# Seven block products for eight in the up projection of a hybrid decoder layer

## The chip, the cores and the metric

The kernel runs on one NeuronCore of one Trainium2 chip. The metric is the device time of one execution in microseconds (us). Its engines have queues of their own and run beside each other: PE (matrix products), DVE and ACT (elementwise work), POOL (elementwise work too), and SP, which here issues the loads. Products are summed in PSUM, 8 banks of 128 x 512 f32; all else lies in SBUF.

## What is computed

One decoder layer on 256 tokens with 2048 features: an input projection, a state-space scan and a windowed attention beside it, an output projection, a feed-forward part with a causal convolution of three taps, and a gate on a projected per-layer embedding. The change is in the last three lines here and in what surrounds them:

```python
h = h + jnp.concatenate([y_ssm, y_att], axis=-1) @ w_out[i]
u = _rmsnorm(h, ffn_norm_g[i]) @ w_up[i]          # 2048 x 11264
u = _causal_dwconv(u, ffn_conv_w[i], ffn_conv_b[i])
g_ff, u_ff = jnp.split(u, [D_FF], axis=-1)        # D_FF = 5632
h = h + (jax.nn.silu(g_ff) * u_ff) @ w_down[i]
gate = jax.nn.sigmoid(_rmsnorm(h, ple_norm_g[i]) @ w_ple_gate[i])
pe = _rmsnorm(p[i] @ w_ple_proj[i], ple_post_g[i])
h = h + gate * pe
```

## The kernel before

Tokens lie in two blocks b of 128. Every f32 product is made of three products in the faster fp32r type: each operand is split into a rounded part hi and the rest lo, and hi x hi, hi x lo and lo x hi are summed in one PSUM bank (`products`, L222 to L224). A weight tile `w` has two K tiles (of 128 rows) by 512 columns, 512 KB, and is loaded by SP (L207, 7 buffers); ACT copies it to `wh` (L192), DVE subtracts to get `wl` (L193); `wh` and `wl` have 4 buffers. One tile feeds 2 K tiles x 2 blocks x 3 = 12 matmuls of 512 columns.

The feed-forward part walks over 11 pairs. A pair is one chunk of 512 gate columns (g) and one of 512 value columns (u). `up(c)` multiplies the left operand `hT` (the residual stream, transposed and scaled by the norm's gain; 16 K tiles) with one chunk's 8 weight tiles, 96 matmuls, into one PSUM pair. ACT scales the rows by `rh` on the way out (L879). Then the chunk is transposed: POOL copies the 16-bit halves of each number apart (`half`, L881), SP starts a DMA transpose to `flip`, POOL puts the halves together (`uc`, L884). ACT and DVE make the convolution (L286, L288: 8 DVE steps a chunk), ACT the SiLU, POOL the product of the two chunks (L904), and ACT and DVE split it into `gT` (`gh`, `gl`).

`project` multiplies `gT` with the rows of w_down for a segment of two pairs (the last has one): 4 column blocks, each in a PSUM pair that DVE adds to the residual `h` (L396). It runs one segment late, behind the ups of the segment that follows. While the output projection w_out ends, `next_lhs` squares the rows of `h` on ACT and transposes them on PE for `hT`; the row scale `rh` is known after the last of them and is applied behind the up. After the last `project`, `embed` makes the embedding's projection (48 matmuls), and the gate projection follows.

Of PSUM, `ps_acc` has two pairs (4 banks) and `ps_tr` two banks through the whole kernel. The order on each engine is made by a scheduler when the kernel is built; only in parts marked by `manual_schedule` PE keeps the order of the code. The queues of DVE, ACT and POOL run strictly in the order given.

## Time and profile before

| | |
|---|---|
| runs | 1434.60, 1434.63, 1436.28 us; median 1434.63 |
| profiled execution, span | 1434.9 us |
| DMA | 292.62 MB, mean 204 GB/s; HBM read 268.32 MB |
| PE busy, slice by slice | over 98% in every stretch of 100 us from 0 to 1300 |
| DVE busy in 100 us | 61 to 82 us |
| POOL busy in 100 us | 12 to 34 us between 600 and 1300, up to 48 in the attention part |
| the feed-forward part | from about 618 to 1317 us, then the embedding and the gate |

How to read the profile's rows: a line of kernel.py, the engine and its operation, what it writes and reads with partitions x elements, the count, then the busy time and the mean of one in ns, then the idle time of the engine just before and who ended it. In a timeline a row begins with its start and its length in us; equal neighbours are merged (x2). The length of an instruction includes what it waits for once it has been started, so the lone length of an operation and its length beside others differ. Matmuls overlap: their distance from start to start tells the rate, not their length.

### The profile page before, as it was taken

The page shows a single profiled execution, that of the slowest core. Times are in us where ns is not written, and L with a number is a line of the kernel's source. Part 1 is how long each engine was busy: PE and PEld are TensorE (multiplying, and loading weights), DVE is VectorE, ACT ScalarE, POOL GpSimd, SP SyncE. Part 2 cuts the span into 40 slices and gives each one's busy share as a digit, 9 for nine tenths or more (in the row PEclk, how much of TensorE's full clock was granted, in tenths as well). Part 3 has the DMA queues.
Part 4 walks back from the last instruction along what each step waited for, and adds up shares of the span by engine and source line. Part 5 has one row for each costly group of instructions (what it writes and reads, how often), then busy time and mean ns, then how long its engine had stood idle before and what let it go on. Part 6 is the DMA issues. An engine that isn't in the chain of part 4 may idle for free.

```text
span 1434.9 us, 18092 instructions
## 1 busy us (share of the span) xinstructions
PE 1423.2 (99%) x6527; PEld 1167.3 (81%) x6527; DVE 984.1 (69%) x1242; ACT 804.2 (56%) x1101; POOL 286.2 (20%) x212
## 2 busy tenths in 40 slices
PE   9999999999999999999999999999999999999998
PEld 7887888888787778888888888888888888888887
DVE  6678876776678897656667646765675576476854
ACT  6675555644567666556556446545554554455643
POOL 0002010008345432013243112201320131120000
PEclk9999999999999999999999999999999999999999
DMA  9656656548687778577887767867876877776671
GB/s 332 236 173 198 215 177 185 171 148 223 188 220 187 209 220 220 168 211 207 219 226 202 217 205 206 225 196 198 230 208 192 223 201 218 206 208 190 208 226 65
DMA packets 163467, 292.62 MB, mean 204 GB/s; under 512 B 93041, under 2 KB 95921, under 8 KB 162993
## 3 DMA queue, kind: packets, MB, share of 16 engines
q1 hardware_dynamic: 162944, 290.99, 70.5%
q8 instruction: 51, 0.84, 0.2%
q10 hardware_dynamic: 432, 0.48, 0.1%
q14 instruction: 40, 0.32, 0.1%
HBM read 268.32 MB, written 2.13 MB: 188 GB/s over the span
## 4 chain that ended last, share of the span: by engine, by line
PE 68%; DVE 1%; ACT 0%; issue 0%; POOL 0%; DVEq 0%; ACTq 0%
PE acc L222 22%; PE acc L224 22%; PE acc L223 22%; PE tr L779 1%; PE tr L272 0%; PE sc L738 0%; DVE wl L193 0%; ACT s L753 0%; DVE nm L749 0%; DVE s L742 0%; ACT wh L192 0%; DVE sg L931 0%; ACT s L761 0%; DVE qkr L672 0%; DVE h L396 0%
## 5 line engine op out<-in xcount | busy, mean ns | idle before, releaser
L193 DVE TENSOR_TENSOR wl<-w,wh 128x1024 fp32r<-128x1024 f32 (+1 forms) x495 | 634.9, 1288 | 378.5 <-ACT wh L192 376.4
L192 ACT CAST wh<-w 128x1024 fp32r<-128x1024 f32 (+1 forms) x495 | 514.8, 1045 | 480.7 <-PE acc L224 431.4
L223 PE MATMUL acc<-wl,ah 128*128 128x512 f32 x1278 | 500.1, 391 | 1.5 <-DVE wl L193 1.5
L224 PE MATMUL acc<-wh,al 128*128 128x512 f32 x1278 | 499.0, 391 | 0.0
L222 PE MATMUL acc<-wh,ah 128*128 128x512 f32 x1278 | 498.3, 392 | 0.0
L223 PEld LDWEIGHTS acc<-wl,ah 128*128 128x128 f32 x1278 | 240.1, 188 | 52.3 <-DVE wl L193 2.4
L222 PEld LDWEIGHTS acc<-wh,ah 128*128 128x128 f32 x1278 | 240.1, 188 | 51.0 <-issue 1.4
L224 PEld LDWEIGHTS acc<-wh,al 128*128 128x128 f32 x1278 | 240.1, 188 | 50.1 <-issue 0.7
L224 PE MATMUL acc<-wh,gl 128*128 128x512 f32 x352 | 137.1, 390 | 0.0
L223 PE MATMUL acc<-wl,gh 128*128 128x512 f32 x352 | 137.1, 390 | 0.0
L222 PE MATMUL acc<-wh,gh 128*128 128x512 f32 x352 | 136.5, 390 | 0.0
L881 POOL COPY half<-u 128x1024 uint16<-128x1024 uint16 x44 | 62.0, 1422 | 264.3 <-ACT u L879 264.3
L222 PE MATMUL acc<-wh,yh 128*128 128x512 f32 x256 | 101.6, 397 | 0.6 <-DVE h L396 0.6
L223 PE MATMUL acc<-wl,yh 128*128 128x512 f32 x256 | 99.9, 390 | 0.0
L224 PE MATMUL acc<-wh,yl 128*128 128x512 f32 x256 | 99.7, 390 | 0.0
L884 POOL COPY uc<-flip 128x1024 uint16<-128x1024 uint16 x44 | 54.9, 1248 | 177.2 <-DMA flip<-half 174.9
L223 PEld LDWEIGHTS acc<-wl,gh 128*128 128x128 f32 x352 | 66.1, 188 | 13.7
L224 PEld LDWEIGHTS acc<-wh,gl 128*128 128x128 f32 x352 | 66.1, 188 | 13.6
L222 PEld LDWEIGHTS acc<-wh,gh 128*128 128x128 f32 x352 | 66.1, 188 | 13.6
L288 DVE SCALAR_TENSOR_TENSOR cv<-uc,fcw,cv 128x254 f32<-128x254 f32 (+1 forms) x176 | 73.2, 476 | 3.4 <-ACT cv L286 3.4
L396 DVE TENSOR_TENSOR h<-h,acc 128x512 f32<-128x512 f32 x112 | 73.0, 678 | 1.8 <-PE acc L224 1.8
L222 PEld LDWEIGHTS acc<-wh,yh 128*128 128x128 f32 x256 | 48.1, 188 | 14.6 <-issue 2.0
(239 smaller groups left out, 1129.2 us busy)
## 6 DMA issues: line engine op xcount, KB each, us to landing
w<-in_w_up_dram SPq DMA_DIRECT2D x176, 512.0 KB, 4.2
w<-in_w_in_dram SPq DMA_DIRECT2D x126, 512.0 KB, 4.2
w<-in_w_down_dram SPq DMA_DIRECT2D x88, 512.0 KB, 4.3
w<-in_w_out_dram SPq DMA_DIRECT2D x64, 512.0 KB, 4.2
w<-in_w_pg_dram SPq DMA_DIRECT2D x32, 512.0 KB, 4.3
seg<-scr SPq DMA_DIRECT2D x8, 512.0 KB, 5.0
xt<-in_xT_dram SPq DMA_DIRECT2D x16, 128.0 KB, 7.0
h<-in_x_dram SPq DMA_DIRECT2D x2, 1024.0 KB, 8.7
```

The costliest lines, as they stand in the source:

```text
L192: S.copy(hi, src)
L193: V.tensor_tensor(out=lo, in0=src, in1=hi.bitcast(F32), op=ALU.subtract)
L222: PE.matmul(acc[b], lhsT=hi, rhs=wh[:, i, :], start=(k == 0), stop=False)
L223: PE.matmul(acc[b], lhsT=hi, rhs=wl[:, i, :], start=False, stop=False)
L224: PE.matmul(acc[b], lhsT=lo, rhs=wh[:, i, :], start=False, stop=(k == total - 1 or (b == NB - 1 and k + 1 == whole)))
L288: V.scalar_tensor_tensor(out=dst[:, s:], in0=ps[:, : T - s], scalar=taps[n - 1 - s], in1=dst[:, s:], op0=ALU.mult, op1=ALU.add)
L396: V.tensor_tensor(out=hs, in0=hs, in1=acc[b], op=ALU.add)
L779: PE.matmul(v3(o[e * HD : (e + 1) * HD, kv * 2 * P : (kv + 1) * 2 * P], 2), lhsT=v[kb][:, vs], rhs=pT[e][:, :, kb, :], start=(kb == 0), st ...
L881: G.tensor_copy(half.rearrange("p (a n) -> p a n", a=2), u_.bitcast(U16).rearrange("p (n a) -> p a n", a=2))
L884: G.tensor_copy(uc[:, :, b * P : (b + 1) * P].bitcast(U16).rearrange("p f (t a) -> p f t a", a=2), flip.rearrange("p (a f) t -> p f t a", ...
```

## The change

The up projection is made for both chunks of a pair at once, in cells of 2 K tiles. For a **mixed** cell the product of 2 token blocks x 2 K tiles with 2 K tiles x 2 chunks is a product of 2 x 2 blocks, and is made with 7 block products in place of 8, each with its three parts: 21 matmuls for 24. The other cells, every second one, are **plain** and keep 8. A pair has 4 of each: 180 matmuls where there were 192.

- The right-hand sums of the mixed cells: `ta` (wu0 - wg0, wu1 - wu0) and `tb` (wu1 - ta0, wg1 - tb0), four subtractions of 128 x 512, on POOL; for the first pair the first of them is on DVE. `wg`, `ta`, `tb` and half of `wu` (`v`) are then split on ACT and DVE.
- The left-hand sums are made once, in `left`, on DVE.
- One up takes all eight PSUM banks (P1, P6, P7, P5 for the mixed cells alone, Q2, Q4, Q3, Q22 for both kinds). Behind it ACT copies P1, and DVE makes eight additions that combine the banks. POOL and SP transpose the results as before.
- The rows are scaled by `rh` before they are transposed (`norm`, then `left`), so that nothing is scaled behind the up. The four `left` steps stand at the start of the part, between plain cells; the embedding's 48 matmuls are put there too, and its result goes to HBM and is read back before the gate.
- Down follows every up, two column blocks each, from the third pair on.
- PE has the order of the code from here to the end. A common pool `ps8` of 8 banks takes the place of `ps_acc` and `ps_tr`.

```diff
-    ps_acc = ctx.enter_context(tc.tile_pool(name="ps_acc", bufs=2, space=PSUM))
-    ps_tr = ctx.enter_context(tc.tile_pool(name="ps_tr", bufs=2, space=PSUM))
+    mixer = ExitStack()
+    ps_acc = mixer.enter_context(tc.tile_pool(name="ps_acc", bufs=2, space=PSUM))
+    ps_tr = mixer.enter_context(tc.tile_pool(name="ps_tr", bufs=2, space=PSUM))
...
+    banks = []
+
+    def bank():
+        return banks[0].tile([P, NC], F32, tag="b", name=nm("b"))
...
+    def load_raw(src):
 
         w = sb(wp, [P, KW, NC], "w", bufs=WR)
+        nc.sync.dma_start(w.rearrange("p a b -> p (a b)"), src)
+        return w
+
+    def split_w(w):
+
         wh = sb(wp, [P, KW, NC], "wh", F32R)
         wl = sb(wp, [P, KW, NC], "wl", F32R)
-        n = kt * NC // pieces
-        w2, wh2, wl2 = (t.rearrange("p a b -> p (a b)") for t in (w, wh, wl))
-        for i in range(pieces):
-            s = slice(i * n, (i + 1) * n)
-            nc.sync.dma_start(w2[:, s], src[:, s])
-            split(w2[:, s], wh2[:, s], wl2[:, s])
+        split(w, wh, wl)
         return wh, wl
+
+    def load_w(src):
+        return split_w(load_raw(src))
...
-    def next_lhs(lhs, ss, n, gain):
+    def squares(ss, n):
 
         for b in range(NB):
             sq = sb(small, [P, NC], "hsq")
             S.activation(out=sq, in_=hres[b][:, n * NC : (n + 1) * NC], func=AF.Square, accum_out=ss[:, b, n : n + 1])
+
+    def next_lhs(lhs, n, gain):
...
-            at[98 + 2 * n] = lambda n=n: next_lhs(hT, ssh, n, g_ffn)
+            at[98 + 2 * n] = lambda n=n: squares(ssh, n)
...
-        next_lhs(hT, ssh, 3, g_ffn)
+        squares(ssh, 3)
...
+        def embed(n):
             acc = acc_pair()
-            gemm(acc, plhs, [w_pe[n, g] for g in range(2 // KW)])
+            gemm(acc, lambda k, b: (ph[:, k, b * P : (b + 1) * P], pl[:, k, b * P : (b + 1) * P]), [w_pe[n, 0]])
             for b in range(NB):
-                pc = pe[b][:, n * NC : (n + 1) * NC]
-                V.tensor_copy(pc, acc[b])
-                sq = sb(small, [P, NC], "hsq")
-                S.activation(out=sq, in_=pc, func=AF.Square, accum_out=ssp[:, b, n : n + 1])
-
-    with tc.tile_pool(name="ffn", bufs=2) as fp:
-
-        def up(c):
-            acc = acc_pair()
-            gemm(acc, hT, [w_up[c, g] for g in range(KT // KW)])
+                t = staged(n % 2 * 2 + b)
+                V.tensor_copy(t, acc[b])
+                nc.scalar.dma_start(pe_d[b, :, n * NC : (n + 1) * NC], t)
...
+        def norm(n):
+            t = sb(fp, [P, NB, NC], f"cv{n % 2}", bufs=1)
+            for b in range(NB):
+                hs = hres[b][:, n * NC : (n + 1) * NC]
+                if n:
+                    S.activation(out=t[:, b, :], in_=hs, func=AF.Copy, scale=rh[:, b : b + 1])
+                else:
+                    V.tensor_scalar_mul(t[:, b, :], hs, rh[:, b : b + 1])
+            normed.append(t)
...
+        def left(n):
+
+            src = normed[n]
+
+            def flip(half):
+                tr = bank().rearrange("p (a t) -> p a t", a=2)
+                for i in range(2):
+                    f = half * 2 + i
+                    for b in range(NB):
+                        PE.transpose(tr[:, i, b * P : (b + 1) * P], src[:, b, f * P : (f + 1) * P], ident)
+                return tr
+
+            tr = flip(1)
+            h, l = (sb(fp, [P, 2, T], f"p{e}{n}", F32R, 1) for e in "hl")
+            for i in range(2):
+                k = 4 * n + 2 + i
+                split(tr[:, i, :], h[:, i, :], l[:, i, :], g_ffn[:, k : k + 1])
+            plain.append((h, l))
+            F = sb(fp, [P, 4, T], "uc", bufs=1).rearrange("p f (a t) -> p (f a) t", a=2)
+            tr = flip(0)
+            for i, dst in ((0, F[:, 0:8:7, :]), (1, F[:, 1:3, :])):
+                k = 4 * n + i
+                S.activation(out=dst, in_=v3(tr[:, i, :], 2), func=AF.Copy, scale=g_ffn[:, k : k + 1])
+            for o, x0, x1, op in ((3, 7, 2, ALU.add), (4, 3, 0, ALU.subtract), (5, 0, 7, ALU.subtract), (6, 1, 4, ALU.subtract)):
+                V.tensor_tensor(out=F[:, o, :], in0=F[:, x0, :], in1=F[:, x1, :], op=op)
+            hi, lo = (sb(act, [P, KG * T], f"a{e}{n}", F32R)[:, : 7 * P].rearrange("p (f t) -> p f t", f=7) for e in "hl")
+            split(F[:, :7, :], hi, lo)
+            mixed.append((hi, lo))
...
+        P1, P6, P7, P5, Q2, Q4, Q3, Q22 = range(8)
+        A11, A12, A22, S1, S2, S3, S4 = range(7)
+
+        def cell_mixed(acc, q, c, first, last, fresh):
+
+            kp = 2 * q
+            wg, wu = (load_raw(w_up[n, kp]) for n in (c, NPAIR + c))
+            ta, tb = (sb(fp, [P, KW, NC], t, bufs=1) for t in ("ta", "tb"))
+            first_sum = G if fresh else V
+            first_sum.tensor_tensor(out=ta[:, 0], in0=wu[:, 0], in1=wg[:, 0], op=ALU.subtract)
+            for o, x0, x1 in ((ta[:, 1], wu[:, 1], wu[:, 0]), (tb[:, 0], wu[:, 1], ta[:, 0]), (tb[:, 1], wg[:, 1], tb[:, 0])):
+                G.tensor_tensor(out=o, in0=x0, in1=x1, op=ALU.subtract)
+            g = split_w(wg)
+            v = [sb(fp, [P, NC], f"v{e}", F32R, 1) for e in "hl"]
+            split(wu[:, 1], *v)
+            a, b = split_w(ta), split_w(tb)
+            right = {P1: (g, 0), Q2: (g, 1), P5: (a, 0), P7: (a, 1), P6: (b, 0), Q4: (b, 1)}
+            hi, lo = mixed[q]
+            left_ = {P1: A11, Q2: A12, Q3: S4, P5: S1, P7: S3, P6: S2, Q4: A22}
+            order = (P1, P5, P7, P6, Q4, Q2, Q3) if first and fresh else (P1, Q2, Q3, P5, P7, P6, Q4)
+            for m in order:
+                f = left_[m]
+                if m == Q3:
+                    r = v
+                else:
+                    w, i = right[m]
+                    r = [t[:, i, :] for t in w]
+                run(acc[m], (hi[:, f, :], lo[:, f, :]), r, first and (fresh or m in (P1, P5, P6, P7)), last and (m in (P1, P5, P6, P7) or not fresh))
+
+        def cell_plain(acc, q, c, first, last, fresh):
+
+            kp = 2 * q + 1
+            h, l = plain[q]
+            for n, out_ in ((c, (Q2, Q4)), (NPAIR + c, (Q3, Q22))):
+                w = load_w(w_up[n, kp])
+                for b, m in enumerate(out_):
+                    for i in range(KW):
+                        bs = slice(b * P, (b + 1) * P)
+                        run(
+                            acc[m],
+                            (h[:, i, bs], l[:, i, bs]),
+                            [t[:, i, :] for t in w],
+                            first and (not fresh or m == Q22) and i == 0,
+                            last and (fresh or m == Q22) and i == KW - 1,
+                        )
...
-                u_ = sb(fp, [P, NC], f"u{b}", bufs=1)
-                S.activation(out=u_, in_=acc[b], func=AF.Copy, scale=rh[:, b : b + 1])
                 half = sb(fp, [P, 2 * NC], f"half{b}", U16, 1)
-                G.tensor_copy(half.rearrange("p (a n) -> p a n", a=2), u_.bitcast(U16).rearrange("p (n a) -> p a n", a=2))
+                G.tensor_copy(half.rearrange("p (a n) -> p a n", a=2), us[b].bitcast(U16).rearrange("p (n a) -> p a n", a=2))
...
+        def up(c, before=None):
+
+            acc = [bank() for _ in range(8)]
+            half = KT // KW // 2
+            cells = [(cell, q) for q in range(half) for cell in (cell_mixed, cell_plain)]
+            if before:
+                cells.sort(key=lambda cq: cq[0] is cell_mixed)
+            for cell, q in cells:
+                if before and cell is cell_plain:
+                    before(q)
+                cell(acc, q, c, q == 0, q == half - 1, not before)
+                if cell is cell_mixed and q == half - 1:
+                    c0, y, x, z = (staged(i) for i in range(4))
+                    S.copy(c0, acc[P1])
+                    V.tensor_tensor(out=x, in0=c0, in1=acc[P6], op=ALU.add)
+                    V.tensor_tensor(out=y, in0=x, in1=acc[P5], op=ALU.add)
+                    V.tensor_tensor(out=x, in0=x, in1=acc[P7], op=ALU.add)
+                    V.tensor_tensor(out=z, in0=x, in1=acc[P5], op=ALU.add)
+            for t, m in ((c0, Q2), (x, Q4), (y, Q3), (z, Q22)):
+                V.tensor_tensor(out=t, in0=t, in1=acc[m], op=ALU.add)
+            cg = finish(c, (c0, x))
+            S.activation(out=cg, in_=cg, func=AF.Silu)
+            cu = finish(NPAIR + c, (y, z))
+            G.tensor_tensor(out=cg, in0=cg, in1=cu, op=ALU.mult)
+            return cg
+
+        def boundary(q):
+            if q == 0:
+                for n in range(3):
+                    embed(n)
+                norm(0)
+                left(0)
+                norm(1)
+                embed(3)
+                left(1)
+            elif q < 3:
+                norm(q + 1)
+                left(q + 1)
+
+        def down(seg, ns, after=None):
+            lhs, i0, ni = seg
+            for n in ns:
+                acc = acc_pair()
+                gemm(acc, lhs, [w_down[i, n] for i in range(i0 * KG // KW, (i0 + ni) * KG // KW)])
+                add_to_h(acc, n)
+                if after:
+                    after(n)
...
-        for s, np_ in enumerate(SEGS):
+        for np_ in SEGS:
             gT = Lhs(fp, KG * np_, "g")
             for i in range(np_):
-                cg = up(pair + i)
-                S.activation(out=cg, in_=cg, func=AF.Silu)
-                cu = up(NPAIR + pair + i)
-                G.tensor_tensor(out=cg, in0=cg, in1=cu, op=ALU.mult)
+                cg = up(pair + i, None if pair + i else boundary)
                 split(cg, gT.t[i][0], gT.t[i][1])
-            if pending:
-                project(*pending.pop())
-            pending.append((gT, w_down, pair, np_))
+                if pending:
+                    down(pending, range(4)[i * 4 // np_ : (i + 1) * 4 // np_])
+            pending = (gT, pair, np_)
...
+        def after(n):
+            squares(ssg, n)
+            if n:
+                next_lhs(h2T, n - 1, g_ple)
+
+        down(pending, range(4), after)
...
+        pe = [sb(lp, [P, D], f"pe{b}", bufs=1) for b in range(NB)]
+        ssp = sb(lp, [P, NB], "ssp", bufs=1)
+        for b in range(NB):
+            nc.scalar.dma_start(pe[b], pe_d[b])
+            sq = sb(lp, [P, D], "sq", bufs=1)
+            S.activation(out=sq, in_=pe[b], func=AF.Square, accum_out=ssp[:, b : b + 1])
+        rp_ = rstd(ssp, D, NB, "rp")
...
+        accs = [acc_pair() for n in range(2)]
+        gate(0, accs[0], range(6))
+        next_lhs(h2T, 3, g_ple)
+        gate(1, accs[1], range(6))
+        for n in range(2):
+            gate(n, accs[n], range(6, 8))
+            end(n, accs[n])
```

In the built order PE has 132 matmuls of 512 columns fewer (3 x 1858 for 3 x 1902), the same 96 transposes, DVE 1375 rows for 1177 and POOL 378 for 205.

POOL, before, in the middle of the feed-forward part: the copies of two chunks of a pair (`u` to `half`, `flip` to `uc`) and the product of the pair (`cv`).

```order
L881 COPY half_1959_9723<-u_1958_9721 128x1024
L881 COPY half_1962_9730<-u_1961_9728 128x1024
L884 COPY uc_9720<-flip_1960_9725 128x4x256
L884 COPY uc_9720<-flip_1963_9732 128x4x256
L881 COPY half_1993_9898<-u_1992_9896 128x1024
L881 COPY half_1996_9905<-u_1995_9903 128x1024
L884 COPY uc_9895<-flip_1994_9900 128x4x256
L884 COPY uc_9895<-flip_1997_9907 128x4x256
L904 TENSOR_TENSOR cv_1964_9735<-cv_1964_9735,cv_1998_9910 128x1024
```

POOL, now, at the same place, behind an up (`c` are the combined results, `w` raw weight tiles of the next up):

```order
L992 COPY half_1583_7361<-c_1572_7311 128x1024
L951 TENSOR_TENSOR ta_7580<-w_7578,w_7576 128x512
L953 TENSOR_TENSOR ta_7580<-w_7578 128x512
L992 COPY half_1585_7366<-c_1574_7313 128x1024
L953 TENSOR_TENSOR tb_7581<-w_7578,ta_7580 128x512
L995 COPY uc_7360<-flip_1584_7363 128x4x256
L992 COPY half_1589_7386<-c_1573_7312 128x1024
L953 TENSOR_TENSOR tb_7581<-w_7576,tb_7581 128x512
L995 COPY uc_7360<-flip_1586_7368 128x4x256
L992 COPY half_1591_7391<-c_1575_7314 128x1024
L951 TENSOR_TENSOR ta_7663<-w_7661,w_7659 128x512
L953 TENSOR_TENSOR ta_7663<-w_7661 128x512
```

Between the copies of one up stand the sums of the first cells of the next one; the first sums of a cell wait behind the first copy, which waits for the up's last matmuls.

DVE, before, within an up: the splits of the weight tiles one after the other, the end of a convolution (`cv`) and the split of a pair's product (`gl`) among them.

```order
L193 TENSOR_TENSOR wl_7747<-w_7745,wh_7746 128x1024
L288 SCALAR_TENSOR_TENSOR cv_1538_7534<-uc_7519,fcw_5460,cv_1538_7534 128x254
L193 TENSOR_TENSOR wl_7765<-w_7763,wh_7764 128x1024
L193 TENSOR_TENSOR wl_7783<-w_7781,wh_7782 128x1024
L193 TENSOR_TENSOR gl_1468_7195<-cv_1504_7359,gh_1467_7194 128x1024
L193 TENSOR_TENSOR wl_7801<-w_7799,wh_7800 128x1024
L193 TENSOR_TENSOR wl_7819<-w_7817,wh_7818 128x1024
```

DVE, now, at the end of an up: the last mixed cell (`vl`, then `wl` from `w`, `ta` and `tb`), the last plain cell, and the first combinations of the banks (`b`), among splits for the down that follows.

```order
L205 TENSOR_TENSOR vl_7279<-w_7266,vh_7278 128x512
L205 TENSOR_TENSOR wl_7275<-w_7264,wh_7274 128x1024
L205 TENSOR_TENSOR wl_7283<-ta_7268,wh_7282 128x1024
L205 TENSOR_TENSOR wl_7287<-tb_7269,wh_7286 128x1024
L205 TENSOR_TENSOR wl_7323<-w_7320,wh_7322 128x1024
L205 TENSOR_TENSOR wl_7341<-w_7338,wh_7340 128x1024
L1019 TENSOR_TENSOR c_1574_7313<-c_1572_7311,b_7008 128x512
L205 TENSOR_TENSOR wl_7417<-w_7414,wh_7416 128x1024
L1020 TENSOR_TENSOR c_1573_7312<-c_1574_7313,b_7010 128x512
L205 TENSOR_TENSOR wl_7435<-w_7432,wh_7434 128x1024
L1024 TENSOR_TENSOR c_1572_7311<-c_1572_7311,b_7011 128x512
```

Two tiles made 24 matmuls with two splits; a mixed cell has three and a half for 21, two of them behind POOL's sums, and the combinations have come to DVE.

More of the change, by code (lines that the diff above doesn't have):

```diff
@@ L119, in fill @@
             G.memset(sb(pool, [P, n // 4], "fill", bufs=1), 0.0)
+    banks = []
+    def bank():
+        return banks[0].tile([P, NC], F32, tag="b", name=nm("b"))
     def acc_pair():
+        if banks:
+            return [bank() for b in range(NB)]
         return [ps_acc.tile([P, NC], F32, tag=f"acc{b}", name=nm(f"acc{b}")) for b in range(NB)]
     def tr_tile():
+        if banks:
+            return bank()
         return ps_tr.tile([P, NC], F32, tag="tr", name=nm("tr"))
@@ L174, in hybrid_layer @@
     S.copy(junk, nhalf[:, :1])
[L176 to L177 removed]
+    scw = sb(mc, [P, 24 * 5], "scw")
+    rw = sb(mc, [P, 256], "rows")
     dtb, alog, dsk, sink = (rw[:, i * 32 : (i + 1) * 32] for i in range(4))
@@ L239, in products, with gemm @@
                         )
-    def gemm(acc, lhs, srcs, halves=False):
+    def gemm(acc, lhs, srcs, halves=False, part=None):
         for s, src in enumerate(srcs):
+            if part is not None and s not in part:
+                continue
             last = s == len(srcs) - 1
@@ L838, in hybrid_layer @@
         fill(as_)
-        next_lhs(hT, ssh, 3, g_ffn)
+        squares(ssh, 3)
     rh = finish_rstd(ssh, "rh")
     mix.close()
-    pp = ctx.enter_context(tc.tile_pool(name="pe", bufs=1))
-    pe = [sb(pp, [P, D], f"pe{b}") for b in range(NB)]
+    mixer.close()
+    banks.append(ctx.enter_context(tc.tile_pool(name="ps8", bufs=8, space=PSUM, reuse_waits="tile")))
+    pp = ctx.enter_context(tc.tile_pool(name="fcw", bufs=1))
     fcw = sb(pp, [P, 88 * 4], "fcw")
@@ new lines, in hybrid_layer @@
+        mixed, plain = [], []
+        def left(n):
[23 more added lines that the diff above has]
+            mixed.append((hi, lo))
@@ L917, in hybrid_layer, with gate, end @@
         pgt = sb(lp, [P, D], "ppg", bufs=1)
-        nc.sync.dma_start(pgt, ppg.partition_broadcast(P))
-        rp_ = finish_rstd(ssp, "rp")
+        nc.scalar.dma_start(pgt, ppg.partition_broadcast(P))
+        pe = [sb(lp, [P, D], f"pe{b}", bufs=1) for b in range(NB)]
[5 more added lines that the diff above has]
+        rp_ = rstd(ssp, D, NB, "rp")
         for b in range(NB):
             V.scalar_tensor_tensor(out=pe[b], in0=pe[b], scalar=rp_[:, b : b + 1], in1=pgt, op0=ALU.mult, op1=ALU.mult)
-        for n in range(4):
-            acc = acc_pair()
-            gemm(acc, h2T, [w_pg[n, g] for g in range(KT // KW)], n == 3)
+        def gate(n, acc, part=None):
+            gemm(acc, h2T, [w_pg[n, g] for g in range(KT // KW)], n == 3, part)
+        def end(n, acc):
             step = NC if n < 3 else NC // 2
@@ L933, in hybrid_layer @@
                     nc.sync.dma_start(out[b][:, ns], sg)
+        accs = [acc_pair() for n in range(2)]
[5 more added lines that the diff above has]
+            end(n, accs[n])
+        for n in range(2, 4):
+            acc = acc_pair()
+            gate(n, acc)
+            end(n, acc)
+    by_hand.__exit__(None, None, None)
     fill(small)
```

46 lines of the change are left out of this document (25 added, 21 removed).

## The prediction

> **What bounds the kernel now.** I read the page's busy shares first, then the stretches of the feed-forward part (the windows view from 640 to 1260 us, which lies wholly in it), then its chain and its waits.
>
> ```profile
> span 1434.9 us, 18092 instructions
> PE 1423.2 (99%) x6527; PEld 1167.3 (81%) x6527; DVE 984.1 (69%) x1242; ACT 804.2 (56%) x1101; POOL 286.2 (20%) x212
> 640.00:1260.00 620.00, 620.00 (x2737) 513.80 (x2736) 396.39 (x437) 324.31 (x373) 142.70 (x92) 1.00 0.77 211
> by line: PE acc L223 33.3%; PE acc L224 33.3%; PE acc L222 33.3%
> DVE wl L193 <- ACT wh L192: 220.3, 168, 3.7
> ACT wh L192 <- PE acc L224: 262.5, 167, 2.0
> ```
>
> In the stretch PE is busy in all 620 us, at a granted clock of 1.00 (third number from the end), and the chain of that stretch is three matmul lines and nothing else. DVE waits 220.3 us for ACT, and ACT 262.5 us for PE to free a buffer: both stand behind PE. So a matmul that goes is worth its full spacing, as long as nobody else becomes slower than PE. Busy time is not that spacing; the starts are (timeline of PE):
>
> ```profile
> 699.78 0.39 PE L222 MATMUL acc<-wh,ah 128*128 128x512 f32 x1
> ...
> 702.50 0.39 PE L223 MATMUL acc<-wl,ah 128*128 128x512 f32 x1
> ```
>
> Twelve matmuls later the start has moved by 2.72 us: 0.227 us a matmul. One up and its share of down is 288 matmuls, 65.3 us; eleven of them make the 718 us of the part.
>
> Next, who could become slower than PE. DVE's and POOL's rows where they meet (two timelines of the same kernel):
>
> ```profile
> 673.86 3.26 POOL L904 TENSOR_TENSOR cv<-cv,cv 128x1024 f32<-128x1024 f32 x1 [5.87 <-DVE cv L288]
> 677.07 4.01 POOL L881 COPY half<-u 128x1024 uint16<-128x1024 uint16 x2
> 676.93 1.28 DVE L193 TENSOR_TENSOR wl<-w,wh 128x1024 fp32r<-128x1024 f32 x1 [2.06 <-ACT wh L192]
> 678.25 1.94 DVE L193 TENSOR_TENSOR gl<-cv,gh 128x1024 fp32r<-128x1024 f32 x1
> 680.11 3.19 DVE L193 TENSOR_TENSOR wl<-w,wh 128x1024 fp32r<-128x1024 f32 x2
> 804.42 3.26 POOL L904 TENSOR_TENSOR cv<-cv,cv 128x1024 f32<-128x1024 f32 x1 [8.44 <-DVE cv L288]
> 804.20 1.22 DVE L193 TENSOR_TENSOR wl<-w,wh 128x1024 fp32r<-128x1024 f32 x1
> 805.34 1.28 DVE L396 TENSOR_TENSOR h<-h,acc 128x512 f32<-128x512 f32 x2
> 806.92 1.85 DVE L193 TENSOR_TENSOR wl<-w,wh 128x1024 fp32r<-128x1024 f32 x1 [0.31 <-ACT wh L192]
> 794.81 1.17 POOL L884 COPY uc<-flip 128x1024 uint16<-128x1024 uint16 x1 [1.92 <-DMA flip<-half]
> 647.58 2.85 DVE L288 SCALAR_TENSOR_TENSOR cv<-uc,fcw,cv 128x255 f32<-128x255 f32 x7
> ```
>
> They **take turns**. POOL's product of 673.86 ends at 677.12; DVE's split, started at 676.93, ends at 678.21, 1.09 us after that; POOL's copy, started at 677.07, ends only at 679.1 (0.89 after the split); DVE's next split ends at 680.19, 1.09 after the copy. So while both have work, a split costs 1.09 and a copy 0.89 us of one common time. At 804 the same: POOL's product begins at 804.42 and lasts 3.26 because DVE's split runs until 805.42, so its own time is 2.26; the split of 806.92 waits until it ends at 807.68 and is over 1.09 later. The two additions between (L396, one input in PSUM, 0.64 each) ran beside it undelayed. So DVE instructions with both inputs in SBUF exclude POOL's; those that read PSUM do not. Now this hardly matters: per 65.3 us of PE, 25 splits (27.3), 16 convolution steps at 0.41 (2.85 for seven, 6.6), 8 PSUM additions (5.1) and POOL's 10.2 (four copies at 0.89, four at about 1.1 by the 1.17 of the lone row, one product of 2.26) are 49.
>
> **The change, part by part.**
>
> *Matmuls.* Each of the 4 mixed cells of an up has 7 products of 3 matmuls in place of 8: 4 x 3 x 11 = 132 fewer, all of 512 columns. 132 x 0.227 = **-29.9 us**. PE's limit is then 1434.9 - 29.9 = 1405.0 for the profiled execution (the runs' median, 1434.63, is the same within 0.3 us, so the sum holds for it too). One up is 180 matmuls, 40.8 us; with a down of 96, 62.6 us.
>
> *What DVE and POOL get for it.* A mixed cell splits wg, ta, tb (1024 columns each) and v (512): 3.5 splits, where its two loads took two. A plain cell takes two, as before. So 22 splits an up in place of 16. POOL makes 16 sums of 512 columns; all of them have both inputs in SBUF. The results leave PSUM by 8 DVE additions (0.64 each, the L396 rows' price) and one ACT copy, where ACT did it alone. No row shows a sum of 512 columns on POOL: half of the product's 2.26 is 1.13; I take 1.1 in turns (bounds: 0.89, the turn of a copy with one input, and 1.3 for a fixed part that doesn't halve).
>
> *A period of one up and one down* (pairs 3 to 10, eight of them), in turns: 31 splits x 1.09 = 33.8; 16 sums x 1.1 = 17.6; the copies and the product 10.2; 16 convolution steps x 0.41 = 6.6; 16 PSUM additions x 0.64 = 10.2; together 78.4 us. Only PSUM additions can stand beside POOL's work. POOL's 27.8 us are some 37% of the time, so I let 37% of 10.2, about 4 us, be hidden: **74.4 us, against PE's 62.6**. PE must wait 11.8 us a period: 8 x 11.8 = **+94 us**. If all 10.2 hide, 68.2 and +45; if none, 78.4 and +126. That DVE's waits for ACT swallow POOL's turns, as they do now, I don't count: those waits end with PE freeing buffers, and go when PE is the one who waits.
>
> *The first three ups* stand without a down between them, so the load is denser. Up 0: 26 splits (four for the embedding) 28.3; the left operands 11 (four times one subtraction of 896 columns, four of 128 and two of 256: about 1.0, 0.8 and 0.95 by their columns); 8 copies from PSUM 5.1; 4 sums on DVE 2.4; 12 sums on POOL 13.2: 60. Ups 1 and 2 each: what ends the up before (8 x 0.64 + 6.6 + 1.1 + 10.2 = 23), 22 splits 24.0 and 16 sums 17.6: 64.6. In all 189, some 6 of them hidden: 183. PE has 588 matmuls and 32 transposes, 136 us. **+47 us** (bounds 25, when the embedding's splits and half the left operands fall before the part, and 61, with none hidden and 8 us at the step from up 1 to up 2, where POOL's next sums stand behind copies that wait for the up's last matmuls). After the last up PE has 288 matmuls of down, 65 us, with little beside them: nothing there.
>
> *What I cost at nothing.* The row scaling needs the last additions into h, squares and POOL's power before the first transpose; 36 matmuls of the embedding (8.2 us) stand ahead of it on PE. Without that cover it would cost about 4 us. The transposes keep their number, 96. The embedding is the same 48 matmuls at another place. Its way through HBM is 2 MB out and 2 MB back beside a DMA share of 0.77 in the row of the stretch; at the end 12 loads' worth of gate matmuls (33 us) stand before its first use, and a load of 1 MB took 8.7 us:
>
> ```profile
> h<-in_x_dram SPq DMA_DIRECT2D x2, 1024.0 KB, 8.7
> ```
>
> PSUM's eight banks are all taken by one up; the next user of a bank finds it read, since the first four are read while the last plain cell runs (5.4 us).
>
> One place in this sum has no row: whether the convolution steps (two inputs in SBUF, but of another form) exclude POOL. In the stretch they ran alone; their mean is that of the undelayed ones:
>
> ```profile
> L288 DVE SCALAR_TENSOR_TENSOR cv<-uc,fcw,cv 128x255 f32<-128x255 f32 x84 | 37.3, 477 | 3.4 <-ACT cv L286 3.4
> ```
>
> I count them as excluding; if they don't, 37% of 6.6 goes too, 2.4 us a period, and the forecast falls by about 26 us. The Trainium skill bears on this, in "SBUF — State Buffer", section "Who interferes with whom": a DVE instruction with two SBUF inputs blocks a GpSimd instruction that reads SBUF, and the other way round, wholly and not in part, whatever the operation. By it the steps exclude POOL and the sum is as it stands; the trace's splits agree (1.00 and 0.76 us of waiting), its convolution steps show nothing.
>
> Sum: 1405.0 + 94 + 47 = **1546 us**.
>
> **The rivals.**
>
> *PE stays the bound* (the other side). POOL's sums fall where DVE waits or reads PSUM, and only the 132 matmuls are seen: 1405 us, faster by 2%. For it: DVE's 220 us of waits, and that 20% of POOL is used. It decides at the point where a period's turns fit in 62.6: without the sums they are 60.8, less 10.2 if every PSUM addition is hidden, so 16 sums would have to cost at most 12.0 us, 0.75 each. The cheapest POOL row of that width, a copy with one input, takes 0.89. Chance 0.12.
>
> *Nearly nothing*: sums as cheap as 0.89 and nearly all PSUM additions hidden. The period is then 64.8, +18 over the eight; with +15 to +25 in the first three about 1440, no change or just slower. Chance 0.04.
>
> *PE loses its clock too.* If PE's waits come in one piece of several us an up, matmuls may start slowly again after each, as they do at the start of the kernel:
>
> ```profile
> 0.84 5.71 PE L155 MATMUL ms<-const-bfloat16-1.0 128*128 128x512 bf16 x13 [0.84 <-PEq L991]
> ```
>
> There thirteen matmuls of the same width took 5.71 us, 0.44 each. Thirteen at 0.44 in place of 0.227 after each of eleven ups would add 2.8 us an up, 30 us: some 1576, and with the upper bounds above 1600. Against it: by my periods the 11.8 us of waiting are spread over some ten splits. Chance 0.05. The Trainium skill, "TensorE: Matmul & The Clock Gate", section "Part 1: The HAM clock gate (the "warmup" mystery)", has the clock halved after an idle window of about 3.4 us; waits of about 1 us would not reach it, and no row of this trace shows an idle of that length before a matmul.
>
> *That the change doesn't do what it says* is out: in the built order PE has 3 x 1858 matmuls of this width where it had 3 x 1902, and POOL has the 172 sums.
>
> **How the numbers follow.** Turns of DVE and POOL set the pace, 1546: 0.79. PE stays the bound, 1405: 0.12. Nearly nothing, about 1440: 0.04. Clock too, 1576 and more: 0.05. The bounds of the first case are 1405 + 45 + 25 = 1475 and 1405 + 126 + 61 = 1592; sums at 0.89 take 172 x 0.21 = 36 us off either, which moves the lower end to about 1445. That range, 1445 to 1595, leaves out the rival that is faster, the one near 1440 and part of the last, some 0.18. A measurement of this kernel tells a change of 0.2%, about 3 us, from none. Faster 0.12, same 0.02, slower 0.86.
>
> **What would show it.** Right: PE's busy share falls in the part, with idle before matmuls ended by DVE's wl; the chain there passes through DVE and POOL in place of three matmul lines; POOL's sums show about 2.2 us each, half of it waiting; DVE's waits for ACT shrink to little; one up and down takes 74 us, and ups 1 and 2 about 64 each. Wrong: matmuls still 0.227 apart throughout (then DVE had room, and the sums cost less than 0.75), or waits ended by DMA or by PSUM being read late, which I priced at nothing.

## The result and the profile after

The changed kernel takes **1562.06 us** in the median of four runs (1561.28 to 1563.43), where the kernel before takes 1435.28 on the same chip (1434.60 to 1436.28). The ratio is 1.0889, with a 95% interval of 1.0874 to 1.0904: 127 us slower. The profiled execution has a span of 1559.6 us.

The page of the kernel after, its busy shares and its chain of waits:

```profile
span 1559.6 us, 18301 instructions
PE 1443.1 (93%) x6395; PEld 1157.4 (74%) x6395; DVE 1267.2 (81%) x1435; ACT 850.1 (55%) x1154; POOL 668.5 (43%) x385
PE 28%; DVE 13%; POOL 8%; issue 5%; ACT 2%; DMA 2%; DVEq 0%; POOLq 0%; ACTq 0%
```

PE has 132 matmuls fewer and is shown busy for 20 us more, which says again that busy time is not pace. It is no longer the bound: DVE and POOL stand in the chain with 13% and 8%, and in the chain of the stretch from 900 to 1300 us, whose lines are these, PE's matmul lines are no longer alone (it runs on with smaller shares):

```profile
by line: DVE cv L305 11.0%; POOL tb L953 10.6%; DVE wl L205 10.0%; PE b L939 8.7%; PE b L940 7.9%; PE b L938 7.3%; issue 6.8%; POOL cv L1028 5.0%; PE b L239 5.0%; PE b L237 5.0%; PE b L238 5.0%; DMA w<-in_w_up_dram 3.4%; DVE vl L205 2.2%; D
```

The settled stretch of the part, from the start of the fifth up to the end of the last, the eleventh (windows view; us, busy time of PE, PEld, DVE, ACT, POOL, granted clock, DMA share, GB/s):

```profile
900.60:1398.10 497.50, 439.80 (x1836) 352.24 (x1835) 442.66 (x413) 250.51 (x292) 333.46 (x166) 0.95 0.61 182
```

Seven ups and six downs, 1836 matmuls. Before, PE was busy in all of its stretch at a clock of 1.00; here it is busy for 439.8 of 497.5 us at 0.95, and DVE for 442.7, 89% of the time. From the starts of the matmuls one up takes 52.2 us and one down 21.5; with the steps between them a **period is 74.2 us** (1345.7 - 900.6 over six). A down runs at PE's own rate (96 x 0.227 = 21.8), so all of the loss is in the ups, 52.2 where their 180 matmuls need 40.8. The groups of DVE and POOL from 900 to 1300 us that the argument was about (line, engine and operation, count, then busy time and mean in ns, then idle time before and who ended it):

```profile
L205 DVE TENSOR_TENSOR wl<-w,wh 128x1024 fp32r<-128x1024 f32 x106 | 158.4, 1514 | 1.1 <-ACT wh L204 0.7
L953 POOL TENSOR_TENSOR tb<-w,ta 128x512 f32<-128x512 f32 x22 | 60.4, 2746 | 21.2 <-DVE wl L205 21.2
L305 DVE SCALAR_TENSOR_TENSOR cv<-uc,fcw,cv 128x255 f32<-128x255 f32 x48 | 46.0, 987 | 0.0
L953 POOL TENSOR_TENSOR ta<-w 128x512 f32<-128x512 f32 x22 | 42.9, 1949 | 0.0
L951 POOL TENSOR_TENSOR ta<-w,w 128x512 f32<-128x512 f32 x22 | 40.8, 1856 | 30.8 <-DMA w<-in_w_up_dram 30.8
L205 DVE TENSOR_TENSOR vl<-w,vh 128x512 fp32r<-128x512 f32 x22 | 28.4, 1292 | 12.0 <-ACT vh L204 12.0
L953 POOL TENSOR_TENSOR tb<-w,tb 128x512 f32<-128x512 f32 x21 | 36.2, 1726 | 0.4
L205 DVE TENSOR_TENSOR gl<-cv,gh 128x1024 fp32r<-128x1024 f32 x5 | 6.1, 1226 | 16.9 <-ACT gh L204 16.9
L205 DVE TENSOR_TENSOR wl<-ta,wh 128x1024 fp32r<-128x1024 f32 x22 | 37.0, 1681 | 6.7 <-ACT wh L204 6.7
L205 DVE TENSOR_TENSOR wl<-tb,wh 128x1024 fp32r<-128x1024 f32 x22 | 34.1, 1552 | 7.9 <-ACT wh L204 7.7
```

Most DVE instructions here that have both inputs in SBUF are longer than they are alone: a split of a raw tile 1514 ns where it takes 1220 undelayed, a convolution step of 255 columns 987 for 477, the half split `vl` 1292 for 690 (the undelayed lengths of splits are in the rows of e3_sums_on_dve below). `gl`, which starts when POOL's product has ended, isn't, and the convolution steps of 254 columns aren't either (471 ns): POOL works beside few of them. The waits of PE for DVE, and of DVE for ACT, in the same 400 us (waits view: total us, times, longest):

```profile
PE b L939 <- DVE wl L205: 33.6, 19, 4.0
DVE wl L205 <- ACT wh L204: 15.1, 21, 1.5
```

DVE's splits wait for ACT for 15.1 us in 400, where it was 220.3 in 620.

### The profile page after: what moved, and what is told of

Its sections match the earlier page's. It is cut to its first block, busy times and chain, and to the rows that moved or that the text cites. A ratio compares the mean times of both kernels' runs of the same rounds, so it can differ in the third digit from the quotient of the medians.

```text
span 1559.6 us, 18301 instructions
## 1 busy us (share of the span) xinstructions
PE 1443.1 (93%) x6395; PEld 1157.4 (74%) x6395; DVE 1267.2 (81%) x1435; ACT 850.1 (55%) x1154; POOL 668.5 (43%) x385
## 4 chain that ended last, share of the span: by engine, by line
PE 28%; DVE 13%; POOL 8%; issue 5%; ACT 2%; DMA 2%; DVEq 0%; POOLq 0%; ACTq 0%
DVE wl L205 6%; PE b L239 5%; PE b L238 5%; PE b L237 5%; DVE cv L305 5%; POOL tb L953 4%; PE b L939 4%; PE b L940 4%; PE b L938 4%; POOL cv L1028 2%; DMA w<-in_w_up_dram 1%; ACT wh L204 1%; DVE vl L205 1%; POOL ta L953 1%; DMA flip<-half 1%
## 5 line engine op out<-in xcount | busy, mean ns | idle before, releaser
L238 PE MATMUL acc<-wl,ah 128*128 128x512 f32 x448 | 176.6, 394 | 0.0
L237 PE MATMUL acc<-wh,ah 128*128 128x512 f32 x448 | 175.8, 395 | 0.0
L239 PE MATMUL acc<-wh,al 128*128 128x512 f32 x448 | 175.6, 392 | 0.0
L939 PE MATMUL b<-wl,ph 128*128 128x512 f32 x352 | 143.3, 407 | 11.2 <-DVE wl L205 11.2
L237 PE MATMUL b<-wh,gh 128*128 128x512 f32 x368 | 144.6, 393 | 4.5 <-ACT gh L204 4.5
L238 PE MATMUL b<-wl,gh 128*128 128x512 f32 x368 | 144.4, 392 | 1.8 <-DVE wl L205 1.8
L239 PE MATMUL b<-wh,gl 128*128 128x512 f32 x368 | 144.1, 392 | 0.0
L938 PE MATMUL b<-wh,ph 128*128 128x512 f32 x352 | 143.3, 407 | 0.0
L940 PE MATMUL b<-wh,pl 128*128 128x512 f32 x352 | 141.3, 401 | 1.5 <-DVE pl L208 1.5
L953 POOL TENSOR_TENSOR tb<-w,ta 128x512 f32<-128x512 f32 x44 | 113.9, 2590 | 36.3 <-DVE wl L205 36.3
```

Of the source, the lines that this page charges most:

```text
L237: PE.matmul(acc[b], lhsT=hi, rhs=wh[:, i, :], start=(k == 0), stop=False)
L238: PE.matmul(acc[b], lhsT=hi, rhs=wl[:, i, :], start=False, stop=False)
L239: PE.matmul(acc[b], lhsT=lo, rhs=wh[:, i, :], start=False, stop=(k == total - 1 or (b == NB - 1 and k + 1 == whole)))
L938: PE.matmul(acc, lhsT=hi, rhs=wh, start=start, stop=False)
L939: PE.matmul(acc, lhsT=hi, rhs=wl, start=False, stop=False)
L940: PE.matmul(acc, lhsT=lo, rhs=wh, start=False, stop=stop)
```

## The experiments

The first theory is that of the prediction: DVE and POOL take turns at SBUF, and the 16 sums an up fill the common time beyond what PE needs. Against it stood that the sums' place in POOL's queue does the harm (they stand behind copies that wait for the up's end), that DVE's own added splits do it, and that PE is still the bound and merely lost its clock. Each run was timed beside runs of the kernel before on its own chip; the ratios are against those.

### Without the sums (e1_no_sums)

```diff
-            ta, tb = (sb(fp, [P, KW, NC], t, bufs=1) for t in ("ta", "tb"))
...
-                G.tensor_tensor(out=o, in0=x0, in1=x1, op=ALU.subtract)
...
-            a, b = split_w(ta), split_w(tb)
+            a, b = split_w(wu), split_w(wg)
```

> Leaves out POOL's 172 sums: ta and tb are not made, the raw tiles wu and wg are split in their place, so PE, ACT and DVE have the same work as in the changed kernel. Turns theory: a period of one up and one down falls from 74 us to PE's 62.6, the first three ups from 190 us to about 142; in all 1405 to 1425 us. Rival 1 (DVE's own added work, 22 splits and 8 additions an up, sets the pace without POOL): stays above 1520. Rival 2 (PE's halved clock in each up): the clock would fall as before and the time stay above 1530.

The edit also leaves out the first pair's four sums on DVE.

Measured: 1446.04 us, ratio 1.0079 [1.0059, 1.0099]; span 1443.9. The windows view of this kernel, over the same seven ups and six downs as the row of after:

```profile
855.70:1282.50 426.80, 420.01 (x1837) 343.98 (x1836) 358.05 (x407) 247.35 (x288) 128.83 (x58) 1.00 0.75 213
```

PE is busy for 420 of 426.8 us, a period is 64.1 us, close to PE's 62.6. DVE has the same splits and is busy for 358 us in place of 442.7, since its instructions wait less for POOL: DVE's added work alone is not what sets the pace, and 116 us of the time hang on the sums. Still, the time is **a miss**: it lies some 20 us above what was expected of the turns, mostly from the start of the part. The first three ups still take about 152 us for PE's 136, and the first down 33.0 for 21.5; in it PE waits 5.39 us for `gh` and 2.54 for `gl`, and its next dozen matmuls start 0.43 us apart in place of 0.227.

### The same sums, but short (e2_short_sums)

All 172 sums stay at their places, with their waits and queues; each covers 32 columns in place of 512. `ta` and `tb` are allocated once and set to zero.

```diff
+        sums = [sb(fp, [P, KW, NC], t, bufs=1) for t in ("ta", "tb")]
...
-                G.tensor_tensor(out=o, in0=x0, in1=x1, op=ALU.subtract)
+                G.tensor_tensor(out=o[:, :32], in0=x0[:, :32], in1=x1[:, :32], op=ALU.subtract)
```

> Same instructions, same queues and the same waits between POOL, ACT, DVE and PE as in the changed kernel, but each sum covers 32 columns of 512 (the rest of ta and tb is zero, so the output isn't the reference's). Turns theory: a sum's turn falls from about 1.17 to about 0.25 us, 16 of them from 18.7 to 4, so a period is PE's 62.6 and the whole 1405 to 1435 us. Rival 3 (not the shared time, but POOL's queue: sums stand behind copies that wait for the up's end and for DMA transposes, and splits behind sums): those waits are all still there, so above 1500.

Measured: 1450.26 us, ratio 1.0108 [1.0088, 1.0129], 15 us above the expected range and far from the rival's 1500; a period is 64.5 us. The short sums are not as short as expected: their means are 0.45 to 0.69 us, waiting included, for the 0.25 that was assumed. POOL's order, its waits for the copies and ACT's wait for `ta` and `tb` are all still there and cost 4 us over leaving the sums out. So the place in POOL's queue is not the cause; the length of the sums is, 112 us of it.

### The sums on DVE (e3_sums_on_dve)

```diff
-            first_sum = G if fresh else V
-            first_sum.tensor_tensor(out=ta[:, 0], in0=wu[:, 0], in1=wg[:, 0], op=ALU.subtract)
+            V.tensor_tensor(out=ta[:, 0], in0=wu[:, 0], in1=wg[:, 0], op=ALU.subtract)
...
-                G.tensor_tensor(out=o, in0=x0, in1=x1, op=ALU.subtract)
+                V.tensor_tensor(out=o, in0=x0, in1=x1, op=ALU.subtract)
```

> All four sums of each cell on DVE, none on POOL; all else the same. Turns theory: a sum costs DVE about 0.6 us and no turn of POOL. A period is 31 splits 33.8 + 16 sums 9.6 + 16 convolution steps 6.6 + 12 PSUM additions 7.7 + POOL's 10.2 = 67.9, less 3 hidden: 65 us against 74, and the first three ups about 165 against 190; 1559.6 - 8 x 9 - 25 = 1455 to 1475 us. Rival 3 (POOL's queue and the handing over between engines): with the hand-overs gone PE is the bound, 1405 to 1420 us. Rival 1 (DVE's own work): DVE gets more of it, so slower than 1560.

Measured: 1537.37 us, ratio 1.0714 [1.0696, 1.0732]: **a miss** by over 60 us, and the rivals' numbers miss as well. A period is 73.2 us, where the turns add up to 65. The windows view, seven ups and six downs:

```profile
882.00:1371.00 489.00, 447.05 (x1838) 354.69 (x1838) 420.02 (x520) 248.90 (x290) 198.61 (x58) 0.95 0.65 186
```

DVE is busy for 420 us and idle for 69, 10.3 us a period; so it isn't DVE's work that fills the period. Two of POOL's rows in one of these ups, and what DVE and ACT do beside the second (timelines of the three engines):

```profile
967.45 12.33 POOL L994 COPY uc<-flip 128x1024 uint16<-128x1024 uint16 x2 [4.48 <-ACT wh L204]
986.48 7.85 POOL L1027 TENSOR_TENSOR cv<-cv,cv 128x1024 f32<-128x1024 f32 x1 [6.69 <-DVE cv L305]
```

```profile
986.24 2.36 DVE L205 TENSOR_TENSOR wl<-w,wh 128x1024 fp32r<-128x1024 f32 x2
988.51 0.69 DVE L205 TENSOR_TENSOR vl<-w,vh 128x512 fp32r<-128x512 f32 x1
989.12 1.22 DVE L205 TENSOR_TENSOR wl<-w,wh 128x1024 fp32r<-128x1024 f32 x1
990.25 0.69 DVE L952 TENSOR_TENSOR tb<-w,ta 128x512 f32<-128x512 f32 x1
990.85 1.22 DVE L205 TENSOR_TENSOR wl<-ta,wh 128x1024 fp32r<-128x1024 f32 x1
995.45 1.23 DVE L205 TENSOR_TENSOR gl<-cv,gh 128x1024 fp32r<-128x1024 f32 x1 [3.37 <-ACT gh L204]
```

```profile
979.82 2.08 ACT L303 ACTIVATE cv<-uc,fcw 128x256 f32<-128x256 f32 x4 [6.17 <-POOL uc L994]
994.36 1.05 ACT L204 CAST gh<-cv 128x1024 fp32r<-128x1024 f32 x1 [5.19 <-POOL cv L1027]
```

POOL's product needs 2.26 us by itself. Here it is started at 986.48, while DVE runs six instructions back to back (986.24 to 992.07), all at their own length: 1.22 for a split, 0.69 for half of one. POOL gets nothing until DVE stops, and ends 2.26 us after that, its own time. They do **not** take turns here; POOL is locked out by a whole run of DVE's. DVE pays for it a moment later: its next instruction is `gl`, which waits for ACT's `gh`, which waits for that product, and the splits that PE needs stand behind it in the queue (3.37 us). The copies of 967.45 to 979.78 do the same to ACT: its convolution waits 6.17 us for `uc`, and behind it stands the cast of `tb` that PE waits for. This was a new theory, and it foretold something: without work on POOL the period must fall to 63 to 65 us.

### And POOL's copies on ACT, its product on DVE (e6_sums_dve_copies_act)

The kernel of e3_sums_on_dve, with POOL idle through the settled part.

```diff
-                G.tensor_copy(half.rearrange("p (a n) -> p a n", a=2), us[b].bitcast(U16).rearrange("p (n a) -> p a n", a=2))
+                S.copy(half.rearrange("p (a n) -> p a n", a=2), us[b].bitcast(U16).rearrange("p (n a) -> p a n", a=2))
...
-            G.tensor_tensor(out=cg, in0=cg, in1=cu, op=ALU.mult)
+            V.tensor_tensor(out=cg, in0=cg, in1=cu, op=ALU.mult)
```

> From e3 (sums on DVE) on: the copies half and uc go from POOL to ACT and the product of the two chunks to DVE, so POOL has nothing in the ups and downs. Theory from e3's trace (POOL's copies wait through whole runs of DVE instructions, and the convolution and gl on DVE then wait for them): DVE's own time is 31 splits 35 + 16 sums 9.6 + convolution 6.6 + 12 PSUM additions 7.7 + product 1.1 = 60 us, under PE's 62.6; a period is 63 to 65 us against e3's 72.4, the whole 1455 to 1475 us. If e3 is slow for DVE's own load or for the hand-overs between DVE and ACT, nothing changes or it gets slower, since both get more: above 1525.

Measured: 1458.07 us, ratio 1.0163 [1.0146, 1.0180]. The windows view, seven ups and six downs:

```profile
868.30:1295.00 426.70, 418.69 (x1837) 343.97 (x1836) 403.52 (x519) 293.59 (x337) 0.00 (x0) 1.00 0.70 212
```

A period is 63.9 us: DVE now does *more* (403.5 us in 426.7, 95%), and PE is back at its pace and at a clock of 1.00. So some 9 us a period in e3_sums_on_dve were POOL's waiting and what stands behind it. That run moved the copies and the product at once; which of the two does more wasn't separated. Most of what is left of the loss lies in the first three ups, 173 us for PE's 136.

### An eighth product back on PE (e4_eighth_back)

```diff
+            run(acc[P1], (hi[:, A11, :], lo[:, A11, :]), [t[:, 0, :] for t in g], first and (fresh or True), False)
```

> Gives PE the 132 matmuls back: in each mixed cell the product P1 is run twice (the output isn't the reference's), the rest unchanged. Turns theory: PE waits 11 us in each up and takes them in its waits; 1555 to 1570 us as without them. Rival 2 (the clock halves because PE waits, and PE is thereby on the path): PE waits less, the clock falls less, and the time falls below 1550 or rises by the matmuls' own 30 us to 1590.

Measured: 1566.92 us, ratio 1.0921 [1.0900, 1.0943]. 132 matmuls, 29.9 us of PE at full clock, cost 4.9 us. So PE has time to spare in the changed kernel, and the matmuls that the change takes out are worth only some 5 us there.

### All cells plain, the rest of the change kept (e5_all_plain)

```diff
-            cells = [(cell, q) for q in range(half) for cell in (cell_mixed, cell_plain)]
...
+            kps = [1, 3, 5, 7, 0, 2, 4, 6] if before else list(range(8))
...
+                cell_plain(acc, kp, c, n == 0, n == 7)
```

> The rest of the change alone: every cell is plain (8 products), no sums; the pool of eight banks, the rows normed before the transposes, the embedding at the front, the downs between the ups all stay. Turns theory: 16 splits an up and no sums are 47 us of DVE's and POOL's common time a period against PE's 65.3, so PE is the bound and only what stands at the step into the part shows, the 4.9 us that PE waits there in the changed kernel: 1435 to 1445 us. Rival 4 (the other edits cost, by PE's fixed order or the later downs): above 1455.

An up takes four banks here, and ACT copies them out.

Measured: 1441.34 us, ratio 1.0048 [1.0033, 1.0063]. The moved embedding, the norm ahead of the transposes, the common pool of banks and the split downs cost 7 us together. PE's timeline where w_out ends and the embedding begins, of this kernel and of after:

```profile
608.56 0.79 PE L237 MATMUL b<-wh,gh 128*128 128x512 f32 x1 [4.40 <-ACT gh L204]
```

```profile
603.51 0.39 PE L239 MATMUL acc<-wh,yl 128*128 128x512 f32 x1
608.39 0.80 PE L237 MATMUL b<-wh,gh 128*128 128x512 f32 x1 [4.50 <-ACT gh L204]
```

ACT's timeline of after gives the reason:

```profile
603.98 0.33 ACTq L881 DMA_DIRECT2D uc<-in_pT_dram  x1
607.72 0.62 ACT L204 CAST gh<-uc 128x512 fp32r<-128x512 f32 x1 [1.01 <-DMA uc<-in_pT_dram]
```

The embedding's left operand is loaded into `uc`, a tile of the feed-forward pool, and that load is issued only at 603.98, half a microsecond after PE's last product; its split comes behind it. From start to start PE's step is 4.88 us (4.79 in e5_all_plain). It costs more than its length: in e5_all_plain the next thirteen matmuls start 0.36 to 0.59 us apart in place of 0.227, while the granted clock of the stretch from 603 to 615 us is 0.72. That is 2.7 us on top of the 4.6 that the step is too long, and the two together are about the 7 us.

### Three attempts at a faster kernel (e7_faster_try, e8_from_fourth, e9_from_third)

e7_faster_try is e6_sums_dve_copies_act with the embedding's operand loaded at the start of the kernel, and a shorter first segment, so that the first down comes earlier:

```diff
-SEGS = [2, 2, 2, 2, 2, 1]
+SEGS = [1, 2, 2, 2, 2, 2]
...
-        pt_ = sb(fp, [P, 4, T], "uc", bufs=1)[:, :2, :]
-        nc.scalar.dma_start(pt_, pT)
+        pt_ = v3(lead[:, : 2 * T], 2)
```

> e6 with the first segment of one pair (the downs begin after the second up) and the embedding's input loaded at the kernel's start. By the same theory the first ups are less dense: 12 to 20 us less than e6, 1440 to 1455 us. If DVE isn't what the first ups wait for, the same as e6.

Measured: 1456.52 us, ratio 1.0155 [1.0140, 1.0170], inside the interval of e6_sums_dve_copies_act, and above what was expected. The wait before the embedding's first matmul fell from 4.41 to 0.76 us, and from the last product of w_out to the end of the fourth up this kernel is 8.1 us shorter than e6_sums_dve_copies_act. Yet a step of 4.43 us, a wait for `gh`, came up before the last segment's products, at 1315, where that segment now has two pairs; with the slow starts behind it, it costs 7.5 us, and gave back what had been won.

e8_from_fourth keeps the early load, has the old segments, and makes the first three ups, those without a down between them, plain: 7 products only from the fourth pair on.

```diff
-                cg = up(pair + i, None if pair + i else boundary)
+                cg = up(pair + i) if pair + i >= FIRST else up_eight(pair + i, None if pair + i else boundary)
```

> From e6: the first three pairs, which have no down ahead of them, are plain (8 products, as in e5, with POOL's copies); the 7 products, sums on DVE and copies on ACT begin with the fourth pair. The embedding's input is loaded at the start. By the theory that the step is decided by DVE's time against PE's in each stretch: the first three ups take PE's 133 us (e5), the eight periods about 63.8 (e6), the step into the part 1 us for 4.8: e5's 1441.3 - 3.7 - 8 x (65.1 - 63.8) = 1427 us, 0.5% faster than the kernel before. If what e6 lost at the front comes back at the fourth pair, 1440 or more.

Measured: 1431.16 us in the median of eight runs (1426.91 to 1431.90), ratio **0.9974** [0.9964, 0.9985]: 0.26% faster than the kernel before, at the edge of what can be told, and 4 us short of the 1427 expected. From the starts of its matmuls the fourth pair's up takes 48.5 us, the later ones 41.8 to 42.9: a part of the loss did come back there. e9_from_third begins with the third pair:

```diff
-FIRST = 3
+FIRST = 2
```

> e8 with the 7 products from the third pair on, whose up follows an up without a down between. The same theory: DVE has some 48 us of work there for PE's 41, less what it is ahead: 2 to 8 us slower than e8, 1429 to 1435 us. If DVE's lead is enough, 2.7 us faster than e8.

Measured: 1433.00 us in ten runs (1430.70 to 1434.57), ratio 0.9995 [0.9986, 1.0004]: no difference from before, within the first range expected.

## Why the prediction was right, and where its steps were off

The forecast was 1546 us, the range 1445 to 1595; the time is 1562.06, and the likeliest case is the one that came. Against the profiled span of 1559.6 the steps stand so:

| step | predicted, us | measured, us |
|---|---|---|
| PE's limit with 132 matmuls fewer | 1405.0 | not reached; the matmuls are gone |
| one period | 74.4 | 74.2 settled, 80 the first |
| eight periods over PE's 62.6 | +94 | 599.8 - 500.8 = +99 |
| the first three ups, over PE's 136 | +47 (183) | +54 (190) |
| the step into the part | 0 | +4.9 |

The measured terms make 1562.9, and the span is 3.3 us less. Of these, 2.4 lie ahead of the part: the 700th of the 800 matmuls of w_out starts at 583.45 us before and at 581.07 after. The rest wasn't placed.

*Matmuls.* The 132 went, and with them nothing of the time, as e4_eighth_back shows from the other side.

*Turns.* Where POOL's sums and DVE's splits alternate, they cost what was foretold. POOL's and DVE's timelines of after:

```profile
1005.61 2.28 POOL L951 TENSOR_TENSOR ta<-w,w 128x512 f32<-128x512 f32 x1
1007.86 2.28 POOL L953 TENSOR_TENSOR ta<-w 128x512 f32<-128x512 f32 x1
1010.09 2.28 POOL L953 TENSOR_TENSOR tb<-w,ta 128x512 f32<-128x512 f32 x1
```

```profile
1006.77 2.20 DVE L205 TENSOR_TENSOR wl<-tb,wh 128x1024 fp32r<-128x1024 f32 x1
1008.89 4.55 DVE L205 TENSOR_TENSOR wl<-w,wh 128x1024 fp32r<-128x1024 f32 x2
```

From sum to sum it is 2.24 us; less the 1.09 of a split, a sum's turn is 1.15, where 1.1 was taken.

*The undecided place*, whether convolution steps exclude POOL, is decided: they do. Alone seven of them took 2.85 us. In after, beside two sums:

```profile
977.06 4.93 DVE L305 SCALAR_TENSOR_TENSOR cv<-uc,fcw,cv 128x255 f32<-128x255 f32 x7
975.93 2.36 POOL L953 TENSOR_TENSOR ta<-w 128x512 f32<-128x512 f32 x1
978.25 1.48 POOL L953 TENSOR_TENSOR tb<-w,ta 128x512 f32<-128x512 f32 x1
```

Seven steps of 255 columns take 2.1 us more. The rule of the Trainium skill, "SBUF — State Buffer", section "Who interferes with whom", that a DVE instruction with two SBUF inputs contends with a GpSimd instruction that reads SBUF, holds for this form too; the trace agrees, by these 2.1 us.

*The period.* That 74.4 lies so near to 74.2 is luck: the terms were off by more. One was mis-sized: I counted 16 PSUM additions a period, 8 for the up and 8 for the down. A down behind every up makes only two column blocks, so it is 8 and 4, and 4 x 0.64 = 2.6 us too much stood in the sum (and in the 49 us of the kernel before). Two other errors are larger, and offset each other:

- *Waiting for POOL.* DVE is busy, its waiting for POOL included, for 442.66 of 497.50 us, 66.0 of the 74.2 of a period. By the rows from 900 to 1300 us some 16 of these are waiting: what the splits, the half splits and the steps of 255 columns took beyond their undelayed lengths is 86 us in 5.4 periods. The sum had charged 23.8 (POOL's 27.8 less the 4 hidden). DVE's own work is then 50, for 50.6 in the sum: the instructions that were counted rightly ran a little longer, which made up for the additions.
- *Idle in order.* The other 8.2 us DVE stands idle in its order: for `gh` behind POOL's product (16.9 us in the 5.4 periods), for `vh` (12.0) and for the casts of `ta` and `tb` (6.7 and 7.9). I had set these waits at nothing, since PE would be the one who waits; the waits for POOL's product I had not seen at all.

The two belong together. In the settled stretch POOL is busy for 51.9 us while DVE stands idle, 7.7 a period: DVE's waits still swallow a part of POOL's turns, which I had not counted, and the waits themselves cost about as much. In e3_sums_on_dve, where the same bookkeeping gave 65 and 73.2 came, the errors don't offset: DVE stands idle for 10.3 us a period there.

*The first three ups* took 190 us in place of 183, some 2.4 of them the slow starts behind the step into the part. By the starts of their matmuls they took 67.9, 64.6 and 57.7 us, where the sum had 60, 64.6 and 64.6, less 6 hidden: here too misses offset each other, and why the first was longer and the third shorter stays open. The windows view of after, from the first up's middle to the end of the third:

```profile
640.00:798.00 158.00, 127.78 (x482) 95.74 (x481) 141.88 (x130) 78.05 (x95) 116.31 (x59) 0.90 0.51 150
```

DVE is busy for 90% of it and POOL for 74%, more than in the settled stretch; e5_all_plain, with plain ups, needs 148 us for the same three. That they are the dense place is what e8_from_fourth rests on.

*The step into the part* was put at nothing, since 36 matmuls of the embedding stand ahead of the first transpose. They do, but they had a load of their own ahead of them that I left out, the moved step's own DMA: 4.9 us, and some 7 with the slow starts behind it.

*The range.* Its lower end was reckoned a little wrong: 1475 - 36 is 1439, not 1445. Nothing hangs on it here.

*The rivals.* PE did not stay the bound. "PE loses its clock too" had 0.05, and its mechanism came: PE's waits are not spread over ten splits, they come in pieces. In the timeline of after:

```profile
988.98 0.39 PE L940 MATMUL b<-wh,al 128*128 128x512 f32 x1
991.63 0.49 PE L938 MATMUL b<-wh,ah 128*128 128x512 f32 x1 [2.27 <-ACT wh L204]
996.17 0.79 PE L939 MATMUL b<-wl,ah 128*128 128x512 f32 x1 [4.04 <-DVE wl L205]
996.76 0.63 PE L940 MATMUL b<-wh,al 128*128 128x512 f32 x1
997.18 0.63 PE L938 MATMUL b<-wh,ah 128*128 128x512 f32 x1
```

After two waits of 2.27 and 4.04 us with one matmul between them the starts are 0.43 us apart. In the trace's clock records the clock of the settled stretch is halved once in each up, for 6.8 or 10.2 us, a part of which PE spends waiting; here seven starts are slow, some 1.5 us. That this costs nearly nothing in the ups is argued, not shown: PE has time over there, since 132 more matmuls cost only 4.9 us (e4_eighth_back), but no run kept the clock full. Where PE is the one that everything waits for, it does cost: 2.7 us at the step into the part in e5_all_plain. So the mechanism was right, and its price in the ups too high.

## What to carry to other kernels

A matmul saved is worth its spacing only as long as what prepares its operands has room; count, for the stretch, DVE's instructions with two inputs in SBUF and POOL's instructions that read SBUF, its copies too, as one common resource, and look for the places where one of them waits in order for the other. Work moved to POOL to relieve a busy DVE can do the reverse: here the length of 172 sums on POOL cost 112 us (e2_short_sums). Moving them to DVE won only 25 us (e3_sums_on_dve); taking POOL's copies and product away as well won 104 of the 127 (e6_sums_dve_copies_act). When a step is moved, its own loads move too: ask where their target is allocated and when it comes free.
